# The channel sub-layer's second product by Strassen's seven products of halves for three of four quarters, and squares on ScalarE

## The chip, the cores and the metric

The kernel runs on one core of a Trainium2 chip. The core has five engines with instruction streams of their own, each worked off in order: TensorE (PE, matmuls; its weight loads are shown apart as PEld), VectorE (DVE), ScalarE (ACT), GpSimd (POOL) and SyncE (SP, which issues the DMAs here). SBUF holds tiles of 128 partitions, PSUM the matmul results. The metric is the device time of one execution in microseconds (us).

## The reference

One layer of an encoder over 512 tokens of width 1024: a mixer (a bidirectional state-space branch and a neighbourhood attention, gated and merged), then the channel sub-layer, each with a residual and a LayerNorm. The change concerns the channel sub-layer alone:

```python
def sq_relu_mlp(x, w1, w2):
    return jnp.square(jax.nn.relu(x @ w1)) @ w2
...
h = layer_norm(DN_ALPHA * h + mix, ln1_g, ln1_b)
h = layer_norm(DN_ALPHA * h + sq_relu_mlp(h, w_ff1, w_ff2), ln2_g, ln2_b)
```

`w_ff1` is 1024 x 4096 and `w_ff2` 4096 x 1024, all in float32.

## The kernel before

**Split products.** Every float32 operand is split in two: `hi`, a Copy on ACT into the type fp32r that PE takes, and `lo`, the value minus `hi`, on DVE. A product is three matmuls that accumulate in one PSUM bank, `mm3`: hi x hi (L352), lo x hi (L353), hi x lo (L354). `weights()` and `split_weights()` load 1 MB of weights by one DMA on SP's queue into a raw tile (`ws`) and split it in two halves of 128x1024: hi on ACT (L341, `wh`), lo on DVE (L342, `wl`). `ws`, `wh` and `wl` have two buffers each, so a slab can be prepared while the one before is in use.

**Stages.** First come the LayerNorm of the input, the mixer and its output product `w_o`; then the second LayerNorm writes the 512 tokens into `acc` (four tiles of 128 tokens x 1024) and, transposed, into `h1Th` and `h1Tl` (channels on the partitions, hi and lo). Then the MLP goes over four quarters `fq` of the 4096 inner channels, 1024 each.

**First product of a quarter** (in the code `ff1`): eight inner tiles `f` of 128 channels. Each takes 8 k-steps x 3 matmuls with `w1` as the stationary operand and the 512 tokens as the moving one: 24 matmuls of 512 columns, 192 a quarter. ACT takes the ReLU from PSUM (L1430, `rl`), DVE multiplies it by the bank to square it (L1431), ACT makes `gh`, the hi of the square (L1432), and DVE `gl`, its lo (L1433). In quarter 0 the first four tiles are worked out early, in two halves of 256 tokens, around the second LayerNorm.

**Second product of a quarter** (`ff2`): for two halves of 512 output columns, 4 token tiles x 8 k-steps x 3 matmuls, 192 a quarter, with `gh`/`gl` as the stationary operand and `w2` as the moving one. DVE adds each of the 8 banks to `acc` (L1463 in quarter 0, where it also scales `acc` by ALPHA; L1467 later). The last quarter is written out apart, token tile by token tile, with the last LayerNorm and the output behind each.

**Beside that** POOL applies the second LayerNorm's scale and shift to `acc` (eight operations of 128x1024, L1439); those of tile 0 are tied behind the first inner tiles by a dependency set by hand. Two rows for the last LayerNorm (`row2`) are loaded ahead of the loop.

**Order.** The mixer's order comes from a planner in the code. In the MLP the framework's scheduler orders each engine's stream when the program is built, from the order in which the operations are written, the buffers and its own estimate of durations; on the chip each engine then follows its stream in order and waits on semaphores. So what a stream has behind a waiting instruction waits too.

Of the kernel before, what the change touches and what calls it, by code (L numbers as in the profile page):

```python
# [35 lines left out]
ALPHA = 2.0 ** 0.25  # L36
# [4 lines left out]
BANKS = {"mm": 2, "tr": 2, "cb": 1, "yd": 1, "so": 2}  # L41
# [271 lines left out]
def encoder_layer(ctx, tc, x, w_in, w_attn_br, w_ssd_br, w_o, w_ff1, w_ff2, pcols, rows64,  # L313
                  d_skip, ln_rows, rpb_pad, consts, lmask, out, dbg=None):
    nc = tc.nc
# [30 lines left out]
    def weights(parts, nk, ncol, name, eng=nc.vector, pool=None, after=None):  # L346
        hi = (pool or wp).tile([P, nk, ncol], F32R, tag="wh", name=f"wh_{name}")
        lo = (pool or wp).tile([P, nk, ncol], F32R, tag="wl", name=f"wl_{name}")
        return split_weights(parts, nk, ncol, name, hi, lo, eng, pool, after)

    def mm3(o, lh, ll, rh, rl, start, stop):
        nc.tensor.matmul(o, lh, rh, start=start, stop=False)  # L352
        nc.tensor.matmul(o, ll, rh, start=False, stop=False)  # L353
        nc.tensor.matmul(o, lh, rl, start=False, stop=stop)  # L354
# [49 lines left out]
    gep = ge.__enter__()  # L404
# [41 lines left out]
    op = plan.op  # L446
# [38 lines left out]
    def load_x(t):  # L485
# [7 lines left out]
       r=[(xts[0].name, 0)], w=[(xts[2].name, 0), ("behind", 0)])  # L493
# [838 lines left out]
    def row(i):  # L1332
        r = gep.tile([P, D], F32, tag="gt", bufs=4, name=f"row{i}")
        nc.sync.dma_start(r, ln_rows[i].partition_broadcast(P))
        return r
# [67 lines left out]
    rx0.__exit__(None, None, None)  # L1403


    row2 = [row(4), row(5)]
    ffp = ctx.enter_context(tc.tile_pool(name="ffp", bufs=1, reuse_waits="tile"))
    NQ = D_FF // D
    for fq in range(NQ):
        last = fq == NQ - 1  # L1410
        gh = ffp.tile([P, KD, S], F32R, tag="gh", bufs=2, name=f"gh{fq}")
        gl = ffp.tile([P, KD, S], F32R, tag="gl", bufs=2, name=f"gl{fq}")
        for s in range(4):
            part = [(w_ff1, 0, fq * D + s * 256, 256)]
            if fq == 0 and s == 2:
                w1 = split_weights(part, KD, 256, "f1_0_2", *third(w3p, "f1_0_2"))
            elif fq or s > 1:
                w1 = weights(part, KD, 256, f"f1_{fq}_{s}")
            for j in range(2):
                f = 2 * s + j  # L1420
                if fq == 0 and s < 2:
                    w1, ps = early[f]
                    ff1_half(w1, j, ps, 1)
                else:
                    ps = psx.tile([P, S], F32, tag="mm", bufs=BANKS["mm"], name=f"ps_f1_{fq}_{f}")
                    for k in range(KD):
# [3 lines left out]
                nc.scalar.activation(rl, ps, AF.Relu)  # L1430
                nc.vector.tensor_tensor(out=rl, in0=rl, in1=ps, op=ALU.mult)  # L1431
                nc.scalar.activation(gh[:, f, :], rl, AF.Copy)  # L1432
                ins = nc.vector.tensor_tensor(out=gl[:, f, :], in0=rl, in1=gh[:, f, :].bitcast(F32),  # L1433
                                              op=ALU.subtract)
                if fq == 0 and f == 4:

                    for t in range(NT):
                        for i, o in ((0, ALU.mult), (1, ALU.add)):
                            aff = nc.gpsimd.tensor_tensor(out=acc[t], in0=acc[t], in1=row1[i], op=o)  # L1439
# [5 lines left out]
        def ff2(ps, t, wh, wl, k0):  # L1445

            ts_ = slice(t * P, (t + 1) * P)
            for k in range(4):
                mm3(ps, gh[:, k0 + k, ts_], gl[:, k0 + k, ts_], wh[:, k, :], wl[:, k, :],
                    k0 + k == 0, k0 + k == KD - 1)  # L1450

        if not last:
            for s in range(2):
                cs = slice(s * 512, (s + 1) * 512)
                pss = [psx.tile([P, 512], F32, tag=tag, bufs=BANKS[tag], name=f"ps_f2_{fq}_{s}_{t}")
                       for t, tag in enumerate(("so", "tr", "so", "tr"))]
                for k0 in (0, 4):
                    w2 = weights([(w_ff2, fq * D + k0 * P, s * 512, 512)], 4, 512, f"f2_{fq}_{s}_{k0}")
                    for t in range(NT):
                        ff2(pss[t], t, *w2, k0)  # L1460
                for t in range(NT):
                    if fq == 0:
                        nc.vector.scalar_tensor_tensor(out=acc[t][:, cs], in0=acc[t][:, cs],  # L1463
                                                       scalar=ALPHA, in1=pss[t], op0=ALU.mult,
                                                       op1=ALU.add)
                    else:
                        nc.vector.tensor_tensor(out=acc[t][:, cs], in0=pss[t], in1=acc[t][:, cs],  # L1467
                                                op=ALU.add)
# [89 lines left out]
```

## Time and profile before

| | |
|---|---|
| median of 3 runs | 1220.36 us (1219.28 to 1220.38) |
| profiled execution | 1219.99 us |
| its span (first to last instruction) | 1217.9 us |
| instructions in all | 16716 |
| granted PE clock, mean | 0.993 |
| DMA | 127.19 MB, mean 104 GB/s |
| loads of `w_ff1` and `w_ff2` | 32 of 1024 KB |
| second product, one of the three matmuls (L352, `gh` x `wh`) | x224, 86.3 us busy |

The profile is one execution on the chip. A busy share is the time in which an engine had an instruction running, over the span; an average over stages with different limits. A group of instructions is one line of the code, one operation and one form of tile: its count, the busy time, the mean length of one in ns, and the idle time of its engine just before, with what ended it. A row of the timeline has the start, the length, and in brackets the idle time before it with its releaser. Busy time counts overlapping ends once; mean lengths don't.

### The profile page before, as it was taken

The page shows a single profiled execution, that of the slowest core. Times are in us where ns is not written, and L with a number is a line of the kernel's source. Part 1 is how long each engine was busy: PE and PEld are TensorE (multiplying, and loading weights), DVE is VectorE, ACT ScalarE, POOL GpSimd, SP SyncE. Part 2 cuts the span into 40 slices and gives each one's busy share as a digit, 9 for nine tenths or more (in the row PEclk, how much of TensorE's full clock was granted, in tenths as well). Part 3 has the DMA queues.
Part 4 walks back from the last instruction along what each step waited for, and adds up shares of the span by engine and source line. Part 5 has one row for each costly group of instructions (what it writes and reads, how often), then busy time and mean ns, then how long its engine had stood idle before and what let it go on. Part 6 is the DMA issues. An engine that isn't in the chain of part 4 may idle for free.

```text
span 1217.9 us, 16716 instructions
## 1 busy us (share of the span) xinstructions
PE 1185.8 (97%) x6378; PEld 1017.4 (84%) x6378; DVE 725.7 (60%) x1361; ACT 563.2 (46%) x946; POOL 491.6 (40%) x540
## 2 busy tenths in 40 slices
PE   5999999999999999999999989999999999999996
PEld 5988898989888888788888878899988888888885
DVE  7748475665666665534889874456654433443556
ACT  4576573836456463324677873432241331331510
POOL 1158967777787776203766720024320000000000
PEclk8999999999999999999999999999999999999998
DMA  6144243333324332234332233263114233322401
GB/s 230 53 143 139 90 136 104 120 109 119 110 98 142 113 110 70 69 104 118 83 87 62 70 129 94 90 222 124 36 69 126 81 104 104 104 91 85 160 28 52
DMA packets 124449, 127.19 MB, mean 104 GB/s; under 512 B 22353, under 2 KB 104913, under 8 KB 124369
## 3 DMA queue, kind: packets, MB, share of 16 engines
q1 hardware_dynamic: 124368, 126.13, 33.4%
q8 instruction: 50, 0.82, 0.3%
q14 instruction: 31, 0.25, 0.1%
HBM read 123.88 MB, written 2.23 MB: 104 GB/s over the span
## 4 chain that ended last, share of the span: by engine, by line
PE 88%; DVE 5%; ACT 3%; issue 2%; POOL 1%; DMA 1%; SPq 0%; DVEq 0%; POOLq 0%; ACTq 0%
PE ps_f L354 9%; PE ps_f L352 9%; PE ps_f L353 9%; PE ps_x L352 5%; PE ps_x L354 5%; PE ps_x L353 5%; PE ps_z L352 3%; PE ps_z L353 3%; PE ps_z L354 2%; PE yd L931 2%; PE ps_sbr L352 2%; PE ps_sbr L354 2%; PE ps_sbr L353 2%; PE ps_g L352 2%; PE ps_g L353 2%
## 5 line engine op out<-in xcount | busy, mean ns | idle before, releaser
L341 ACT ACTIVATE wh_f<-ws_f 128x1024 fp32r<-128x1024 f32 x60 | 60.1, 1052 | 118.6 <-PE ps_f L353 96.4
L740 DVE SCALAR_TENSOR_TENSOR cv<-ps_x,pc,cv 128x511 f32<-128x511 f32 (+1 forms) x128 | 95.7, 748 | 25.8 <-ACT cv L732 22.1
L353 PE MATMUL ps_f<-h1Th,wl_f 128*128 128x512 f32 (+1 forms) x288 | 104.6, 366 | 0.0
L352 PE MATMUL ps_f<-h1Th,wh_f 128*128 128x512 f32 (+1 forms) x288 | 104.4, 366 | 0.0
L354 PE MATMUL ps_f<-h1Tl,wh_f 128*128 128x512 f32 (+1 forms) x288 | 103.1, 367 | 1.0 <-DVE h1Tl L428 1.0
L342 DVE TENSOR_TENSOR wl_f<-ws_f,wh_f 128x1024 fp32r<-128x1024 f32 x60 | 72.7, 1251 | 45.3 <-ACT wh_f L341 45.1
L353 PE MATMUL ps_f<-wh_f,gl 128*128 128x512 f32 x224 | 86.8, 389 | 0.0
L354 PE MATMUL ps_f<-wl_f,gh 128*128 128x512 f32 x224 | 86.5, 389 | 0.0
L352 PE MATMUL ps_f<-wh_f,gh 128*128 128x512 f32 x224 | 86.3, 389 | 0.0
L352 PE MATMUL ps_z<-wh_z,hTh 128*128 128x256 f32 x256 | 75.9, 296 | 0.0
L354 PE MATMUL ps_z<-wl_z,hTh 128*128 128x256 f32 x256 | 72.4, 283 | 0.0
L353 PE MATMUL ps_z<-wh_z,hTl 128*128 128x256 f32 x256 | 72.4, 283 | 0.0
L1431 DVE TENSOR_TENSOR rl<-rl,ps_f 128x512 f32<-128x512 f32 x32 | 21.7, 687 | 69.1 <-ACT rl L1430 68.9
L1047 DVE TENSOR_TENSOR ysacc<-ps_sbr,ysacc 128x512 f32<-128x512 f32 x56 | 38.4, 688 | 40.4 <-PE ps_sbr L354 39.9
L354 PEld LDWEIGHTS ps_f<-h1Tl,wh_f 128*128 128x128 f32 x288 | 53.3, 188 | 9.9 <-DVE h1Tl L428 1.2
L352 PEld LDWEIGHTS ps_f<-h1Th,wh_f 128*128 128x128 f32 x288 | 54.1, 188 | 8.9
L353 PEld LDWEIGHTS ps_f<-h1Th,wl_f 128*128 128x128 f32 x288 | 54.2, 188 | 8.6
L1430 ACT ACTIVATE rl<-ps_f 128x512 f32<-128x512 f32 x32 | 19.0, 597 | 89.1 <-PE ps_f L354 85.6
L352 PE MATMUL ps_x<-hTh,wh_bc 128*128 128x512 f32 (+1 forms) x144 | 57.1, 396 | 1.6 <-ACT wh_bc L470 1.6
L352 PE MATMUL ps_sbr<-yTh,wh_sbr 128*128 128x512 f32 x128 | 55.8, 436 | 1.1 <-DVE ysacc L1047 0.5
L353 PE MATMUL ps_x<-hTh,wl_bc 128*128 128x512 f32 (+1 forms) x144 | 54.1, 376 | 2.0 <-POOL wl_bc L473 2.0
L1319 POOL TENSOR_TENSOR gt<-gt,ysacc 128x512 f32<-128x512 f32 x8 | 12.8, 1599 | 106.3 <-ACT gt L1059 98.1
(301 smaller groups left out, 3677.3 us busy)
## 6 DMA issues: line engine op xcount, KB each, us to landing
ws_f<-in_w_ff SPq DMA_DIRECT2D x32, 1024.0 KB
bc<-acs_d SPq DMA_DIRECT2D x32, 512.0 KB
ws_bc<-in_w_in SPq DMA_DIRECT2D x16, 512.0 KB
ws_x<-in_w_in SPq DMA_DIRECT2D x8, 1024.0 KB
ws_z<-in_w_in SPq DMA_DIRECT2D x8, 1024.0 KB
ws_g<-in_w_in SPq DMA_DIRECT2D x8, 1024.0 KB
ws_sbr<-in_w_ssd_br SPq DMA_DIRECT2D x8, 1024.0 KB
ws_qk<-in_w_in SPq DMA_DIRECT2D x16, 512.0 KB
```

Of the source, the lines that this page charges most:

```text
L341: nc.scalar.activation(hi[:, k], st[:, k], AF.Copy)
L342: (eng[i] if isinstance(eng, tuple) else eng).tensor_tensor(out=lo[:, k], in0=st[:, k], in1=hi[:, k].bitcast(F32), op=ALU.subtract)
L352: nc.tensor.matmul(o, lh, rh, start=start, stop=False)
L353: nc.tensor.matmul(o, ll, rh, start=False, stop=False)
L354: nc.tensor.matmul(o, lh, rl, start=False, stop=stop)
L740: op("DVE", 0.75, lambda j=j, o=o, n=n: nc.vector.scalar_tensor_tensor(out=acc()[:, o], in0=ps()[:, n], scalar=tap(j), in1=acc()[:, o], op ...
L931: nc.tensor.matmul(yd()[:, c % 2, h * HD : (h + 1) * HD], bc()[:, 1, h, :], xtok()[:, c, h * HD : (h + 1) * HD], start=True, stop=True)
L1047: op("DVE", 0.69, lambda d=d, ps=ps: nc.vector.tensor_tensor(out=ysacc[:, d, :], in0=ps(), in1=ysacc[:, d, :], op=ALU.add), r=[(ps.name, 0 ...
L1319: nc.gpsimd.tensor_tensor(out=g1, in0=g1, in1=ysacc[:, d, :], op=ALU.mult)
L1430: nc.scalar.activation(rl, ps, AF.Relu)
L1431: nc.vector.tensor_tensor(out=rl, in0=rl, in1=ps, op=ALU.mult)
```

## The change

**Seven products.** For quarters 0 to 2 the second product, a (512 x 1024) times b (1024 x 1024), is cut into halves on all three sides: a(m, i), two token halves and two halves of the inner channels; b(i, n), two inner and two output halves. Eight products of halves are replaced by Strassen's seven, written in the order 3, 6, 4, 2, 1, 5, 7. Each is 4 k-steps x 2 token tiles x 3 matmuls of 512 columns, 24; the bank of a product is added to or subtracted from `acc` at one or two places (`into`, L1492 and L1495): 24 operations a quarter instead of 8, on DVE.

**Left operands.** The square is kept as float32 (`r2`): ReLU on ACT (L1551), then Square on ACT (L1553); `gh` and `gl` are gone. Five of the seven left operands are sums or differences of halves of r2 (`total`, L1438, on DVE, tile `as_`), all seven are split: hi on ACT (L1443), lo on DVE (L1444). They rotate through four pairs of buffers (`blocks`, `wh_blocks`/`wl_blocks`).

**Right operands.** `w2` of a quarter is loaded raw as two tiles of 2 MB by four DMAs (L1427, `w2r_0` and `w2r_1`). Five of the seven right operands are sums (`total`, on POOL, two of 128x1024 each; into tiles `wt_` or in place in `w2r`), all seven are split into `wh` and `wl`, the buffers that the `w1` slabs use too.

**The rest.** `row2` is loaded behind the loop. The last quarter keeps its work.

```diff
+    blocks = ffp.tile([P, 2, 2, 4, 256], F32R, tag="gl", bufs=1, name="blocks")
+    pairs = [(blocks[:, i, 0], blocks[:, i, 1]) for i in range(2)]
...
+    def ff2_strassen(fq, r2):
+        w = [ffp.tile([P, KD, 512], F32, tag="wr", bufs=2, name=f"w2r_{fq}_{n}") for n in range(2)]
...
+        b = {(i, n): w[n][:, 4 * i : 4 * i + 4, :] for i in range(2) for n in range(2)}
+        a = {(m, i): r2[:, 4 * i : 4 * i + 4, m * 256 : (m + 1) * 256] for m in range(2)
+             for i in range(2)}
+        halves = (slice(0, 2), slice(2, 4))
+        def total(dst, x, y, op, eng):
+            for d, k in zip(dst, halves):
+                eng.tensor_tensor(out=d, in0=x[:, k], in1=y[:, k], op=op)
+            return dst
+        def split(hi, lo, src):
+            for x, k in zip(src, halves):
+                nc.scalar.activation(hi[:, k], x, AF.Copy)
+                nc.vector.tensor_tensor(out=lo[:, k], in0=x, in1=hi[:, k].bitcast(F32),
+                                        op=ALU.subtract)
...
+        def left(name, x, y=None, op=ALU.add):
+            hi, lo = pairs[turn[0] % len(pairs)]
+            turn[0] += 1
...
+            t = ffp.tile([P, 4, 256], F32, tag="asum", bufs=1, name=f"as_{fq}_{name}")
+            return split(hi, lo, total(cut(t), x, y, op, nc.vector))
+        def right(name, x, y=None, op=ALU.add, dst=None):
...
+                x = total(cut(dst), x, y, op, nc.gpsimd)
...
+            return split(wp.tile([P, 4, 512], F32R, tag="wh", name=f"wh_f2_{fq}_{name}"),
+                         wp.tile([P, 4, 512], F32R, tag="wl", name=f"wl_f2_{fq}_{name}"), x)
...
+        def product(pss, l, r):
+            for k in range(4):
+                for j, ps in enumerate(pss):
+                    ts_ = slice(j * P, (j + 1) * P)
+                    mm3(ps, l[0][:, k, ts_], l[1][:, k, ts_], r[0][:, k, :], r[1][:, k, :],
+                        k == 0, k == 3)
...
+        product(p3, left("3", a[0, 0]), right("3", b[0, 1], b[1, 1], sub))
+        into(p3, 0, 1)
+        into(p3, 1, 1)
...
+        product(p6, left("6", a[1, 0], a[0, 0], sub), right("6", b[0, 1], b[0, 0], dst=b[0, 1]))
+        into(p6, 1, 1)
...
+        product(p4, left("4", a[1, 1]), right("4", b[1, 0], b[0, 0], sub))
...
+        product(p2, left("2", a[1, 0], a[1, 1]), right("2", b[0, 0]))
...
+        r5 = right("5", b[1, 1])
...
+        product(p1, left("1", a[0, 0], a[1, 1]), right("1", b[0, 0], b[1, 1], dst=b[0, 0]))
...
+        product(p5, left("5", a[0, 0], a[0, 1]), r5)
...
+        product(p7, left("7", a[0, 1], a[1, 1], sub), right("7", b[1, 0], b[1, 1], dst=b[1, 0]))
+        into(p7, 0, 0)
...
                 nc.scalar.activation(rl, ps, AF.Relu)
-                nc.vector.tensor_tensor(out=rl, in0=rl, in1=ps, op=ALU.mult)
-                nc.scalar.activation(gh[:, f, :], rl, AF.Copy)
-                ins = nc.vector.tensor_tensor(out=gl[:, f, :], in0=rl, in1=gh[:, f, :].bitcast(F32),
-                                              op=ALU.subtract)
+                if not last:
+                    ins = nc.scalar.activation(r2[:, f, :], rl, AF.Square)
```

Where the instructions stand now is seen at three places. In the rows an engine's stream is listed in order: line, operation, output <- inputs, and the shape; x2 means two in a row. Lines are those of the changed code.

POOL in quarter 0, where before nothing stood behind the last pair of `acc` (there L1439). The number behind `wt_` is the product, the last number only tells buffers apart:

```order
L1563 TENSOR_TENSOR acc_7632<-acc_7632,row_7621 128x1024
L1438 TENSOR_TENSOR wt_3_0_8672<-w2r_1_8661 128x1024
L1438 TENSOR_TENSOR wt_3_1_8673<-w2r_1_8661 128x1024
L1563 TENSOR_TENSOR acc_7632<-acc_7632,row_7623 128x1024
L1438 TENSOR_TENSOR wt_4_0_8759<-w2r_0_8660 128x1024
L1438 TENSOR_TENSOR w2r_1_8661<-w2r_1_8661,w2r_0_8660 128x1024 x2
L1438 TENSOR_TENSOR wt_4_1_8760<-w2r_0_8660 128x1024
L1438 TENSOR_TENSOR w2r_0_8660<-w2r_0_8660,w2r_1_8661 128x1024 x4
```

The first of these rows still waits for the square of inner tile 4; the ten sums of the quarter's right operands stand between and behind the last two rows of `acc`. The `w2r_1` rows are the right operand of product 6, the `w2r_0` rows those of 7 and 1.

DVE in quarter 0, from the second left operand's sum to the first accumulations (`r_0` is r2 of quarter 0, `wl_f_0_6` the lo of product 6's right operand):

```order
L1438 TENSOR_TENSOR as_2_8799<-r_0_8413 128x512
L1444 TENSOR_TENSOR wl_blocks<-r_0_8413,wh_blocks 128x512
L1444 TENSOR_TENSOR wl_blocks<-as_2_8799,wh_blocks 128x512
L1444 TENSOR_TENSOR wl_f_0_3_8677<-wt_3_0_8672,wh_f_0_3_8676 128x1024
L1444 TENSOR_TENSOR wl_f_0_3_8677<-wt_3_1_8673,wh_f_0_3_8676 128x1024
L1438 TENSOR_TENSOR as_2_8799<-r_0_8413 128x512
L1444 TENSOR_TENSOR wl_blocks<-r_0_8413,wh_blocks 128x512
L1444 TENSOR_TENSOR wl_blocks<-as_2_8799,wh_blocks 128x512
L1438 TENSOR_TENSOR as_1_8848<-r_0_8413 128x512 x2
L1444 TENSOR_TENSOR wl_f_0_6_8722<-w2r_1_8661,wh_f_0_6_8721 128x1024
L1492 SCALAR_TENSOR_TENSOR acc_7632<-acc_7632,ps_f_0_3_0_8666 128x512
L1492 SCALAR_TENSOR_TENSOR acc_7634<-acc_7634,ps_f_0_3_0_8666 128x512
```

The stretch of DVE's stream ahead of the first accumulations before:

```order
L1431 TENSOR_TENSOR rl_5_8605<-rl_5_8605,ps_f_0_5_8580 128x512
L1433 TENSOR_TENSOR gl_8417<-rl_4_8567,gh_8416 128x512
L1433 TENSOR_TENSOR gl_8417<-rl_5_8605,gh_8416 128x512
L1431 TENSOR_TENSOR rl_6_8643<-rl_6_8643,ps_f_0_6_8618 128x512
L1433 TENSOR_TENSOR gl_8417<-rl_6_8643,gh_8416 128x512
L1431 TENSOR_TENSOR rl_7_8673<-rl_7_8673,ps_f_0_7_8648 128x512
L342 TENSOR_TENSOR wl_f_0_0_4_8739<-ws_f_0_0_4_8740,wh_f_0_0_4_8738 128x1024 x2
L1433 TENSOR_TENSOR gl_8417<-rl_7_8673,gh_8416 128x512
L342 TENSOR_TENSOR wl_f_0_1_0_8803<-ws_f_0_1_0_8804,wh_f_0_1_0_8802 128x1024 x2
L1463 SCALAR_TENSOR_TENSOR acc_7632<-acc_7632,ps_f_0_0_0_8678 128x512
```

Ahead of product 6's lo now stand ten operations that read two SBUF tiles, eight of 512 columns and two of 1,024.

PE in quarter 1, where product 5 begins (`ps_f_1_5_0` is its first bank; `wh_f_1_5`, `wh_f_1_1` the right operands):

```order
L354 MATMUL ps_f_1_2_1_9366<-wl_f_1_2_9375,wh_blocks 128x512
L352 MATMUL ps_f_1_5_0_9459<-wh_f_1_5_9408,blocks 128x512
L352 MATMUL ps_f_1_5_1_9460<-wh_f_1_5_9408,blocks 128x512
L352 MATMUL ps_f_1_1_0_9414<-wh_f_1_1_9425,wh_blocks 128x512
L353 MATMUL ps_f_1_1_0_9414<-wh_f_1_1_9425,wl_blocks 128x512
L352 MATMUL ps_f_1_1_1_9415<-wh_f_1_1_9425,wh_blocks 128x512
L353 MATMUL ps_f_1_1_1_9415<-wh_f_1_1_9425,wl_blocks 128x512
L353 MATMUL ps_f_1_5_0_9459<-wh_f_1_5_9408,blocks 128x512
L354 MATMUL ps_f_1_5_0_9459<-wl_f_1_5_9409,blocks 128x512
L353 MATMUL ps_f_1_5_1_9460<-wh_f_1_5_9408,blocks 128x512
L354 MATMUL ps_f_1_5_1_9460<-wl_f_1_5_9409,blocks 128x512
```

Products 5 and 1 are interleaved; before, PE went through one bank after the other with the same three kinds. ACT's stream for the same stretch (`as_5`, `as_7` are left operands, `wh_f_2_0` is `w1` of quarter 2):

```order
L1443 ACTIVATE wh_f_1_5_9408<-w2r_1_9229 128x1024 x2
L1443 ACTIVATE blocks<-as_5_9461 128x512
L1443 ACTIVATE wh_f_1_1_9425<-w2r_0_9228 128x1024 x2
L1443 ACTIVATE blocks<-as_5_9461 128x512
L1443 ACTIVATE blocks<-as_7_9498 128x512 x2
L1443 ACTIVATE wh_f_1_7_9507<-w2r_0_9228 128x1024 x2
L341 ACTIVATE wh_f_2_0_9540<-ws_f_2_0_9542 128x1024 x2
```

Every hi of the late products stands on ACT in the order of this list, and the next quarter's first `w1` behind product 7's.

More of the change, by code (lines that the diff above doesn't have):

```diff
@@ L1360, in ff1_half, with third @@
                 h1Th[:, k, c], h1Tl[:, k, c], k == 0, k == KD - 1)
-    def third(pool, name):
-        return [pool.tile([P, KD, 256], F32R, tag=n, name=f"{n}_{name}") for n in ("wh3", "wl3")]
+    def third(pool, name, shape=[P, KD, 256]):
+        return [pool.tile(shape, F32R, tag=n, name=f"{n}_{name}") for n in ("wh3", "wl3")]
     wos = []
@@ L1403, in encoder_layer, with ff2 @@
     rx0.__exit__(None, None, None)
-    row2 = [row(4), row(5)]
     ffp = ctx.enter_context(tc.tile_pool(name="ffp", bufs=1, reuse_waits="tile"))
     NQ = D_FF // D
+    blocks = ffp.tile([P, 2, 2, 4, 256], F32R, tag="gl", bufs=1, name="blocks")
+    pairs = [(blocks[:, i, 0], blocks[:, i, 1]) for i in range(2)]
+    turn = [0]
+    def ff2(ps, t, wh, wl, k0):
+        ts_ = slice(t * P, (t + 1) * P)
+        for k in range(4):
+            mm3(ps, gh[:, k0 + k, ts_], gl[:, k0 + k, ts_], wh[:, k, :], wl[:, k, :],
+                k0 + k == 0, k0 + k == KD - 1)
@@ L1409, in encoder_layer @@
     for fq in range(NQ):
         last = fq == NQ - 1
-        gh = ffp.tile([P, KD, S], F32R, tag="gh", bufs=2, name=f"gh{fq}")
-        gl = ffp.tile([P, KD, S], F32R, tag="gl", bufs=2, name=f"gl{fq}")
+        if last:
+            gh = ffp.tile([P, KD, S], F32R, tag="gh", bufs=1, name="gh3")
+            gl = ffp.tile([P, KD, S], F32R, tag="gl", bufs=1, name="gl3")
+        else:
+            r2 = ffp.tile([P, KD, S], F32, tag="gh", bufs=1, name=f"r2_{fq}")
         for s in range(4):
@@ L1430, in encoder_layer @@
                 nc.scalar.activation(rl, ps, AF.Relu)
-                nc.vector.tensor_tensor(out=rl, in0=rl, in1=ps, op=ALU.mult)
-                nc.scalar.activation(gh[:, f, :], rl, AF.Copy)
-                ins = nc.vector.tensor_tensor(out=gl[:, f, :], in0=rl, in1=gh[:, f, :].bitcast(F32),
-                                              op=ALU.subtract)
+                if not last:
+                    ins = nc.scalar.activation(r2[:, f, :], rl, AF.Square)
+                else:
+                    nc.vector.tensor_tensor(out=rl, in0=rl, in1=ps, op=ALU.mult)
+                    nc.scalar.activation(gh[:, f, :], rl, AF.Copy)
+                    nc.vector.tensor_tensor(out=gl[:, f, :], in0=rl, in1=gh[:, f, :].bitcast(F32),
+                                            op=ALU.subtract)
                 if fq == 0 and f == 4:
@@ L1443, in encoder_layer @@
                                     reason="behind the first channels")
[L1445 to L1450, printed above, removed]
-        if not last:
[L1453 to L1468, printed above, removed]
+        if not last:
+            if fq == 0:
+                third_pair = third(w3p, "blocks", [P, 2, 4, 256])
+                pairs += [tuple(x[:, i] for x in third_pair) for i in range(2)]
+            ff2_strassen(fq, r2)
     r0 = (NQ - 1) * D
-    w2h = ffp.tile([P, KD, 512], F32R, tag="gh", bufs=2, name="w2h")
-    w2l = ffp.tile([P, KD, 512], F32R, tag="gl", bufs=2, name="w2l")
+    w2h = ffp.tile([P, KD, 512], F32R, tag="wr", bufs=2, name="w2h")
+    w2l = ffp.tile([P, KD, 512], F32R, tag="wr", bufs=2, name="w2l")
     for k0 in (0, 4):
@@ L1477, in encoder_layer @@
              [weights([(w_ff2, r0 + k0 * P, 512, 512)], 4, 512, f"f2_3_1_{k0}") for k0 in (0, 4)]]
+    row2 = [row(4), row(5)]
     for t in range(NT):
```

49 lines of the change are left out of this document (added).

## The prediction, as it was put on record

> **What bounds the kernel now.** I read the page's busy shares and its chain first, then the waits of TensorE (PE) alone over the last part of the program, from 660 us on, which holds the channel sub-layer, and last the windows of that stage.
>
> ```profile
> PE 1185.8 (97%) x6378; PEld 1017.4 (84%) x6378; DVE 725.7 (60%) x1361; ACT 563.2 (46%) x946; POOL 491.6 (40%) x540
> POOL 1158967777787776203766720024320000000000
> PE 88%; DVE 5%; ACT 3%; issue 2%; POOL 1%; DMA 1%; SPq 0%; DVEq 0%; POOLq 0%; ACTq 0%
> PE ps_f L354 <- DVE h1Tl L428: 1.0, 1, 1.0
> 900.00:940.00 40.00, 40.00 (x179) 33.10 (x178) 14.85 (x17) 10.28 (x12) 2.67 (x2) 1.00 0.26 79
> 940.00:980.00 40.00, 40.00 (x178) 33.14 (x177) 16.46 (x21) 11.72 (x16) 0.00 (x0) 1.00 0.34 105
> 953.10 0.60 ACT L1430 ACTIVATE rl<-ps_f 128x512 f32<-128x512 f32 x1 [3.65 <-PE ps_f L354]
> 958.54 0.60 ACT L1430 ACTIVATE rl<-ps_f 128x512 f32<-128x512 f32 x1 [3.46 <-PE ps_f L354]
> ```
>
> PE is busy 97% of the span and makes 88% of the last chain. The digits are POOL's busy tenths in 40 slices of 30.4 us: it does nothing from 913 us on. The wait row is the only one on the MLP's banks (waited, times, longest): 1.0 us, once, at its start. The windows (length, PE, PEld, VectorE (DVE), ScalarE (ACT), GpSimd (POOL), clock, DMA share, GB/s) show PE full at clock 1.00 while DVE works 15 of 40 us. So in the MLP the time is the matmul count times one spacing. Two ReLUs, each behind 24 matmuls, start 5.44 us apart: 0.2267 us per matmul.
>
> **What it removes.** Seven products of 4 k-steps x 2 token tiles x 3 terms are 168 matmuls where a quarter had 192. Three quarters save 72 x 0.2267 = 16.3 us, 5.44 each, all on the path.
>
> As a figure only: the Trainium skill (TensorE: Matmul & The Clock Gate, Back-to-back issue gap) gives about 131 ns for a sustained 512-column matmul. By it the 72 would save 9.4 us and the sum below would end some 7 us later; the two ReLU rows show 226.7 ns here.
>
> **What it adds: prices.**
>
> ```profile
> L342 DVE TENSOR_TENSOR wl_f<-ws_f,wh_f 128x1024 fp32r<-128x1024 f32 x60 | 72.7, 1251 | 45.3 <-ACT wh_f L341 45.1
> L341 ACT ACTIVATE wh_f<-ws_f 128x1024 fp32r<-128x1024 f32 x60 | 60.1, 1052 | 118.6 <-PE ps_f L353 96.4 <-PE ps_o L353 22.1
> L1433 DVE TENSOR_TENSOR gl<-rl,gh 128x512 fp32r<-128x512 f32 x32 | 21.7, 687 | 8.6 <-ACT gh L1432 8.4
> L1432 ACT ACTIVATE gh<-rl 128x512 fp32r<-128x512 f32 x32 | 19.9, 627 | 9.3 <-DVE rl L1431 9.1
> L1467 DVE TENSOR_TENSOR acc<-ps_f,acc 128x512 f32<-128x512 f32 x16 | 11.0, 689 | 22.7 <-PE ps_f L354 22.7
> L1305 POOL TENSOR_TENSOR acc<-acc,rows 128x1024 f32<-128x1024 f32 x2 | 4.8, 2402 | 0.0
> 300.04 5.19 POOL L473 TENSOR_TENSOR wl_bc<-ws_bc,wh_bc 128x1024 fp32r<-128x1024 f32 x2
> 301.32 1.64 DVE L917 TENSOR_TENSOR bc<-bc,amd 128x512 f32<-128x512 f32 x1
> 884.76 3.11 DVE L342 TENSOR_TENSOR wl_f<-ws_f,wh_f 128x1024 fp32r<-128x1024 f32 x1
> 877.07 9.72 POOL L1439 TENSOR_TENSOR acc<-acc,row 128x1024 f32<-128x1024 f32 x4 [20.36 <-PE tp_h L422]
> 883.33 1.28 DVE L1431 TENSOR_TENSOR rl<-rl,ps_f 128x512 f32<-128x512 f32 x2 [1.17 <-ACT rl L1430]
> ```
>
> Busy time over count (60.1 / 60 = 1.00, 72.7 / 60 = 1.21) counts overlapping ends once and is what a step of an unbroken row costs. I take for such a step: DVE 1.18 for a 1,024 lo (some of the 60 were held by POOL), 0.65 for a 512-column sum, lo or accumulation; ACT 1.0 and 0.61; POOL 2.40 for a 1,024 sum. Per quarter the MLP had on DVE 16 lo of weights, 16 half-size squares and lo and 8 accumulations, 16 x 1.18 + 24 x 0.65 = 34.5; it gets 8 lo for w1, 14 lo and 10 sums of r2 halves, 14 lo of w2 and 24 accumulations: 22 x 1.18 + 48 x 0.65 = 57.2, beside 360 x 0.2267 = 81.6 us of PE. ACT goes from 26 to some 40: 22 hi of 1.0, 14 of 0.61, eight ReLU and eight Squares of 0.6. POOL, idle before, gets 10 x 2.40 = 24. That fits as an average; but most of DVE's part is due inside the 38 us of the seven products, and DVE and POOL disturb each other. The left sums read r2 in pieces of 256 columns, which no row of this form shows; the 512-column lo at 0.69 bounds them above, 0.65 is taken.
>
> **Turns.** Two POOL operations with DVE's `bc` between them took 5.19, not 2 x 2.40: 0.39 more; and the 512-column `bc` took 1.64, not 0.65. A lo that started at 884.76 ended at 887.87, 1.08 behind the end of POOL's four (886.79). So a DVE operation with two SBUF inputs waits until a running POOL sum ends, and the next POOL sum waits for it: **they go by turns**. A 512-column one costs POOL 0.4; a 1,024 one 1.18 less the same overlap of 0.25, 0.93 (estimate). DVE operations that read PSUM are not held: at 883.33 two ran in 1.28 during POOL's four. The accumulations are thus free of this, the left sums and all lo are not.
>
> **Quarter 0.**
>
> ```profile
> 883.51 0.40 PE L352 MATMUL ps_f<-h1Th,wh_f 128*128 128x512 f32 x1
> 882.70 1.09 ACT L1430 ACTIVATE rl<-ps_f 128x512 f32<-128x512 f32 x2 [4.96 <-PE ps_f L354]
> L1430 ACT ACTIVATE rl<-ps_f 128x512 f32<-128x512 f32 x32 | 19.0, 597 | 89.1 <-PE ps_f L354 85.6 <-DVE gl L1433 3.5
> ```
>
> Inner tile f4 starts at 883.51; by the new order 90 matmuls lie between it and product 3, 903.9; product 6 is due at 909.35, and its third kind of matmul, which needs the lo of its right sum, four matmuls later, 910.25. POOL's stream begins with acc's last affine pair, behind the Square of f4 on ACT. ACT from 882.70: two ReLU 1.1, two w1 hi 2.0, two Squares 1.2, two ReLU 1.2, four short ones 2.45 and four more 2.45 with that Square: 893.1. Ahead of right 6's lo, DVE's order has ten two-SBUF operations (eight of 512 columns, two of 1,024), and POOL has ten operations ready (the pair of acc, two sums each of right 3, 4 and 6, and right 7's two, which wait only for POOL itself): 10 x 2.40 + 8 x 0.4 + 2 x 0.93 = 29.1, so 922.2. The lo ends at 923.4, PE has it 0.1 later: **13.25 late** for 910.25. Behind that lo stand, on DVE, the accumulations of product 3 and the lo of left 1 and right 4; only PE waits for them, later than for this one, since PE itself stands. From there PE and DVE run side by side, DVE late again at three places. The second half of right 6's lo stands behind four accumulations and a left lo: 923.4 + 2.6 + 0.65 + 1.18 = 927.9, due 16 matmuls on, 927.1: +0.8. Then DVE has 5.6 us of right 4, left 1, left 5's sums and product 6's accumulations (933.4), right 2 2.36, left 5's two lo around one POOL turn for right 1's sum 0.65 + 2.4 + 0.65, product 4's four accumulations 2.6, and right 5's lo 1.18: 943.2, where PE comes at 940.6: +2.7. Right 1's lo by the same count: 949.5 for 948.65, +0.85. Lag of quarter 0: **17.6**. From below it is 2, if the turns let right 6 through: seven POOL sums before it end the sixth at 907.5, and 1.0 + 1.2 for hi and lo give 909.7.
>
> **Quarters 1 and 2.** POOL's sums lie in the 43 us of the first product there, in which DVE has 8 lo of w1 (9.4) and some 11 of the first products' halves; I take them as hidden. With t = 0 at product 3's start, DVE's work is unbroken from 5.65 (first accumulation): 4 accumulations 2.60, one lo 0.65, right 4 2.36, left 1 sums 1.30, 2 accumulations 1.30, right 2 2.36, left 1 lo 1.30 with one POOL turn 2.40, 4 accumulations 2.60, half of left 5's sum 0.65: 23.17. Its hi on ACT ends at 23.8, product 5 is due at 4 x 5.44 = 21.76: **+2.0**. Right 1's hi stands behind it on ACT, 24.8, and PE, two matmuls on, wants it at 24.2: +0.6. Then DVE: right 5's lo 2.36, the sum's other half 0.65, left 5's lo 0.65: 26.8, four matmuls on was 25.7, +1.1; product 2's four accumulations 2.60 and right 1's lo 1.18, 30.6, twelve matmuls on was 29.6, +1.0. Product 7's right hi needs the wh slot of product 5, which the new order of PE ends last, directly before product 7: ACT 1.0 and the handover, +1.3. The next quarter's first w1 hi stands behind product 7's two hi on ACT, while PE has four matmuls (0.9) to spare: 2.05, +1.15. Sum **7.15** a quarter, 14.3 for two; from below 4.9 if DVE keeps up with products 5 and 1, from above 12 if the turns also hold back w1's lo.
>
> **What is hidden.** Eight Squares per quarter cost ACT 0.60 each in place of a Copy of 0.63; DVE's multiply goes; both lie beside 43 us of PE. No Square is in the trace: between 0.60 and 0.69, eight times, nothing either way.
>
> ```profile
> 932.00:933.00 1.00, 1.00 (x6) 0.81 (x6) 0.00 (x0) 0.00 (x0) 0.00 (x0) 1.00 1.02 342
> 933.00:934.00 1.00, 1.00 (x6) 0.84 (x5) 0.00 (x0) 0.00 (x0) 0.00 (x0) 1.00 0.95 337
> 715.00:720.00 5.00, 2.28 (x16) 1.77 (x15) 2.61 (x12) 2.81 (x5) 0.23 (x1) 1.00 0.14 51
> 720.00:725.00 5.00, 5.00 (x16) 3.94 (x15) 5.00 (x9) 5.00 (x9) 0.00 (x0) 0.66 0.92 352
> ```
>
> The 4 MB of raw w2 per quarter move at 340 GB/s, 12.3 us, within 43 of the first product; the w1 slab behind them in SP's queue keeps 6 us or more. If that cover went, it would be 3 us a slab. Behind a pause PE runs slower for a while: the window after 715 to 720 has 16 matmuls at clock 0.66, where 24 would fit, 1.8 us. After quarter 0's pause DVE sets the pace, so I add 0 (to 1). The last quarter keeps its work; row2's later load has tens of us.
>
> Sum, from this execution's 1219.99 (span 1217.9 and 2.1 around it; the median shown is 0.4 more): -16.3 + 17.6 + 14.3 = +15.6, **1236**.
>
> **Rivals.** *The sums get out of the way* (faster): no more than 2 in quarter 0 and 4.9 in each other, 11.8 - 16.3 = -4.5, 1215.5; all of it hidden, 1203.7. For it: POOL idles for the whole MLP after its affine, and DVE half of it. Against: ten turns ahead of one lo, in DVE's fixed order. It is decided by right 6's lo, before or after 910.25. *The turns reach the first product* (slower still): in quarters 1 and 2 eight POOL sums fall among w1's lo, f4's and f6's, with a slack near one turn; +5 each, 1246. For it: DVE is held 2.4 at a time; against: PE is then 24 matmuls per tile behind. *Cancelled*: quarter 0 loses about as much as the two floors allow, lag 16.3, 1220. That the saving is not made is out: the order has 168 matmuls a quarter.
>
> **How the numbers follow.** Forecast 0.48, faster 0.27 (1204 to 1217), cancelled 0.10, slower still 0.15. The forecast alone would be 1229 to 1241. The range, 1211 to 1246, leaves out the lower part of the faster case and what lies above the slowest. A measurement of this kernel tells 0.2%, 2.4 us, from no change: faster 0.27, same 0.09, slower 0.64.
>
> **What would show it.** In the profile after: a wait of PE of some 13 us in quarter 0 near 910 on DVE's lo of right 6 (L1444), DVE and POOL rows there alternating with held lengths of 2.4 and more; waits of 1 to 2 us in each later quarter at products 5, 1 and 7; spacing still 0.2267. Wrong if POOL's sums and DVE's lo overlap at their short lengths, if right 6 is ready in time, or if the first products of quarters 1 and 2 wait.

## The result, and the profile after

The changed kernel takes 1232.40 us (median of 5 runs, 1228.54 to 1235.33) where the kernel before took 1220.38 beside it; the ratio is 1.0091, 95% interval 1.0072 to 1.0111. It is **slower by 12 us** (0.9%), though it has 72 matmuls fewer. Its profiled execution took 1232.32, with a span of 1230.5. The page's lines that answer to those of before:

```profile
PE 1177.5 (96%) x6306; PEld 1004.0 (82%) x6306; DVE 836.4 (68%) x1451; ACT 605.4 (49%) x1006; POOL 579.1 (47%) x570
POOL 1158968777787776204766700043391612702000
PE 76%; DVE 16%; ACT 3%; issue 3%; DMA 1%; POOL 0%; SPq 0%; DVEq 0%; ACTq 0%; POOLq 0%
```

PE has its 72 matmuls less (6306 for 6378), DVE 111 us more of busy time (in which its waiting for POOL counts), and POOL now works behind 913 us, where it had been idle. In the last chain DVE went from 5% to 16%. PE's waits from 884 us on, which were 1.0 us in all before (waited, times, longest), first those of quarter 0, then those of quarters 1 and 2:

```profile
PE ps_f L354 <- DVE wl_f L1444: 10.1, 3, 9.4
PE ps_f L352 <- ACT wh_f L1443: 1.8, 1, 1.8
PE ps_f L352 <- DVE acc L1492: 1.5, 2, 1.1
PE ps_f L354 <- DVE h1Tl L428: 1.1, 1, 1.1
...
PE ps_f L352 <- ACT rl L1551: 1.3, 1, 1.3
PE ps_f L354 <- DVE wl_f L1444: 1.0, 2, 0.5
PE ps_f L353 <- DVE wl_blocks L1444: 0.7, 1, 0.7
PE ps_f L353 <- DVE blocks L1444: 0.7, 1, 0.7
...
```

One wait stands out: 9.4 us for a right operand's lo, in quarter 0. To size the whole I take the stage from the start of inner tile f4 to the last matmul, since what lies ahead of it has the same instructions in the same order in both kernels and yet ended between 881.5 and 886.9 in the profiles of this study. In the timeline (start, length), the last matmul of before, then both ends of after:

```profile
1208.37 0.39 PE L354 MATMUL ps_f<-wl_f,gh 128*128 128x512 f32 x1
...
885.20 0.40 PE L352 MATMUL ps_f<-h1Th,wh_f 128*128 128x512 f32 x1
1220.91 0.39 PE L354 MATMUL ps_f<-wl_f,gh 128*128 128x512 f32 x1
```

The stage took 1208.37 - 883.51 = 324.86 before and 335.71 after, 10.85 more; 1.7 of the span's 12.6 lie ahead of it, where nothing was changed. With the saving of 16.3 made, PE lost 27.2 us in it. Summing what each row of PE starts later than the matmuls ahead of it explain at 0.2267 each: 18.9 in quarter 0, 3.3 in the products of quarter 1, 1.6 at one ReLU in the first product of quarter 2, 3.3 in its products.

**The turns.** POOL, DVE and PE in quarter 0, and last POOL and DVE in quarter 1:

```profile
894.07 2.48 POOL L1563 TENSOR_TENSOR acc<-acc,row 128x1024 f32<-128x1024 f32 x1 [5.61 <-ACT r L1553]
896.51 5.66 POOL L1438 TENSOR_TENSOR wt<-w2r 128x1024 f32<-128x1024 f32 x2
917.13 5.54 POOL L1438 TENSOR_TENSOR w2r<-w2r,w2r 128x1024 f32<-128x1024 f32 x2
...
899.84 2.89 DVE L1444 TENSOR_TENSOR wl_blocks<-as,wh_blocks 128x512 fp32r<-128x512 f32 x1
902.65 6.75 DVE L1444 TENSOR_TENSOR wl_f<-wt,wh_f 128x1024 fp32r<-128x1024 f32 x2
917.75 5.48 DVE L1438 TENSOR_TENSOR as<-r 128x512 f32<-128x512 f32 x2
923.15 1.21 DVE L1444 TENSOR_TENSOR wl_f<-w2r,wh_f 128x1024 fp32r<-128x1024 f32 x1
...
924.41 1.22 PE L354 MATMUL ps_f<-wl_f,blocks 128*128 128x512 f32 x2 [9.36 <-DVE wl_f L1444]
943.19 0.47 PE L352 MATMUL ps_f<-wh_f,blocks 128*128 128x512 f32 x1 [1.10 <-DVE acc L1492]
...
1020.39 6.83 POOL L1438 TENSOR_TENSOR w2r<-w2r,w2r 128x1024 f32<-128x1024 f32 x2 [32.71 <-DVE wl_f L1444]
1021.30 1.29 DVE L1444 TENSOR_TENSOR wl_blocks<-as,wh_blocks 128x512 fp32r<-128x512 f32 x2
1022.50 2.47 DVE L1495 TENSOR_TENSOR acc<-acc,ps_f 128x512 f32<-128x512 f32 x4
```

From 897 on each 512-column sum or lo of DVE takes 2.7 to 2.9 us as long as POOL has sums. Accumulations, which read PSUM, are not held: in quarter 1 four of them take 2.47, 0.6 each, while POOL's two sums run. POOL's ten end at 917.13 + 5.54 = 922.67, 28.6 after they began; the next DVE row, right 6's lo, takes 1.21, and PE goes on as it ends. The window of that quarter's seven products (length, PE, PEld, DVE, ACT, POOL, clock, DMA share, GB/s):

```profile
905.60:962.60 57.00, 43.56 (x170) 33.61 (x169) 56.79 (x53) 19.91 (x25) 23.20 (x8) 0.85 0.18 63
```

PE works 43.6 of 57.0 us in it and DVE, its waiting for POOL counted as busy, 56.8.

### The profile page after: what moved, and what is told of

It reads as the page before. It is cut to its first block, busy times and chain, and to the rows that moved or that the text cites. A ratio compares the mean times of both kernels' runs of the same rounds, so it can differ in the third digit from the quotient of the medians.

```text
span 1230.5 us, 16770 instructions
## 1 busy us (share of the span) xinstructions
PE 1177.5 (96%) x6306; PEld 1004.0 (82%) x6306; DVE 836.4 (68%) x1451; ACT 605.4 (49%) x1006; POOL 579.1 (47%) x570
## 4 chain that ended last, share of the span: by engine, by line
PE 76%; DVE 16%; ACT 3%; issue 3%; DMA 1%; POOL 0%; SPq 0%; DVEq 0%; ACTq 0%; POOLq 0%
PE ps_f L354 7%; PE ps_f L352 7%; PE ps_f L353 7%; PE ps_x L352 5%; PE ps_x L354 5%; PE ps_x L353 4%; DVE wl_f L1444 3%; PE ps_z L352 3%; PE ps_z L353 2%; PE ps_z L354 2%; PE yd L931 2%; PE ps_sbr L352 2%; PE ps_sbr L354 2%; PE ps_sbr L353 2%; PE ps_g L352 2%
## 5 line engine op out<-in xcount | busy, mean ns | idle before, releaser
L1438 POOL TENSOR_TENSOR w2r<-w2r,w2r 128x1024 f32<-128x1024 f32 x18 | 56.2, 3147 | 77.6 <-DVE wl_f L1444 77.6
L342 DVE TENSOR_TENSOR wl_f<-ws_f,wh_f 128x1024 fp32r<-128x1024 f32 x36 | 51.0, 1447 | 20.1 <-ACT wh_f L341 20.1
L352 PE MATMUL ps_x<-hTh,wh_x 128*128 128x512 f32 (+1 forms) x144 | 55.1, 383 | 0.0
L1438 POOL TENSOR_TENSOR wt<-w2r 128x1024 f32<-128x1024 f32 x12 | 31.7, 2665 | 49.3 <-DMA w2r<-in_w_ff 49.3
L354 PE MATMUL ps_x<-hTl,wh_bc 128*128 128x512 f32 (+1 forms) x144 | 54.2, 376 | 0.2 <-DVE hTl L585 0.2
L341 ACT ACTIVATE wh_f<-ws_f 128x1024 fp32r<-128x1024 f32 x36 | 36.1, 1052 | 36.8 <-PE ps_o L353 22.1
L473 POOL TENSOR_TENSOR wl_bc<-ws_bc,wh_bc 128x1024 fp32r<-128x1024 f32 x15 | 37.5, 2518 | 35.3 <-ACT wh_bc L470 35.2
```

What stands on the lines that cost most here:

```text
L341: nc.scalar.activation(hi[:, k], st[:, k], AF.Copy)
L342: (eng[i] if isinstance(eng, tuple) else eng).tensor_tensor(out=lo[:, k], in0=st[:, k], in1=hi[:, k].bitcast(F32), op=ALU.subtract)
L473: op(e, us, lambda k=k, eng=eng: eng.tensor_tensor(out=wl()[:, k], in0=ws()[:, k], in1=wh()[:, k].bitcast(F32), op=ALU.subtract), r=keys + ...
L1438: eng.tensor_tensor(out=d, in0=x[:, k], in1=y[:, k], op=op)
```

## The experiments

Each kernel was timed beside the kernel before on the same chip, and the table has its stage as above, from its own profile. "Saved" is 0.2267 per matmul left out, "lost" is the stage less 324.86 and more the saving. The stage varies less than the time: two profiles of one kernel (eight_dve_p1 and eight_dve_p1_again) took 1213.10 and 1210.29, and have it at 316.37 and 316.45.

| run | time, before beside it | ratio, 95% | stage | saved | lost |
|---|---|---|---|---|---|
| the change | 1232.40, 1220.38 | 1.0072 to 1.0111 | 885.20 to 1220.91: 335.71 | 16.3 | 27.2 |
| q0_sums_dve | 1225.69, 1220.86 | 1.0028 to 1.0055 | 885.98 to 1216.67: 330.69 | 16.3 | 22.1 |
| affine_early | 1232.23, 1220.86 | 1.0063 to 1.0117 | 883.90 to 1219.39: 335.49 | 16.3 | 26.9 |
| q0_no_sums | 1218.31, 1220.86 | 0.9950 to 0.9981 | 886.85 to 1210.61: 323.76 | 16.3 | 15.2 |
| q0_eight | 1225.22, 1220.86 | 1.0014 to 1.0040 | 881.50 to 1211.01: 329.51 | 10.9 | 15.5 |
| eight_late | 1217.80, 1221.65 | 0.9956 to 0.9980 | 884.15 to 1206.44: 322.29 | 10.9 | 8.3 |
| eight_late_p1 | 1213.22, 1221.65 | 0.9913 to 0.9950 | 885.20 to 1203.10: 317.90 | 10.9 | 3.9 |
| eight_dve_p1 | 1210.99, 1221.65 | 0.9892 to 0.9929 | 885.30 to 1201.67: 316.37 | 10.9 | 2.4 |
| squares_alone | 1221.68, 1221.65 | 0.9989 to 1.0013 | 884.66 to 1209.52: 324.86 | 0 | 0 |
| seven_dve_p1 | 1218.40, 1220.94 | 0.9966 to 0.9989 | 884.16 to 1206.85: 322.69 | 16.3 | 14.1 |
| after_p1 | 1227.06, 1220.94 | 1.0030 to 1.0064 | 881.60 to 1211.58: 329.98 | 16.3 | 21.4 |

**Quarter 0's sums on DVE** (`sums` stands in `right` where `nc.gpsimd` stood):

```diff
+        sums = nc.vector if fq == 0 else nc.gpsimd
```

> The ten right sums of quarter 0 go from POOL to DVE, nothing else in the text; DVE gets 10 x 1.2 = 12 us more in that quarter and shares nothing with POOL there. Theory (turns): PE's 9.4 us wait for right 6's lo goes, since without turns its lo follows its sums at once, near 912; the quarter's lag falls from 19 to 3 to 5 us: 1217 (1214 to 1221). Rival (DVE is simply overfull): 12 us more on DVE make the quarter later still, 1232 to 1244. If the turns matter but DVE is as full, between: 1224 to 1230.

1225.69, in the band between the two. PE's two largest waits in this kernel's MLP:

```profile
PE ps_f L352 <- ACT blocks L1444: 5.0, 2, 4.6
PE ps_f L354 <- DVE wl_f L1445: 2.6, 4, 1.0
```

No lo is waited for by more than 1.0, and the stage is 5.0 us shorter although DVE does ten operations more; but left 5, whose sum stands behind all of DVE's other work, is now 4.6 late. So the turns did cost, and DVE is full too.

**The affine pair earlier**

```diff
+                if fq == 0 and f == 0:
+                    first = ins
...
-                                tc.add_manual_dep(aff.ins, ins.ins.name, mybir.DependencyInfo(
+                                tc.add_manual_dep(aff.ins, first.ins.name, mybir.DependencyInfo(
```

> The dependency that holds acc's last affine pair, and with it all sums behind it in POOL's stream, is tied to inner tile f0 in place of f4: POOL starts at about 888.8 in place of 894.1, with the same ten operations. Theory (the lo of right 6 comes when ten turns are through): all of the 5.3 us come off PE's wait, 1227 (1225.5 to 1229). Rival (the last left sums wait for inner tile f7 at 906.5 and five turns are due behind it, whenever POOL starts): under 1 us, 1231.5 to 1233.

1232.23, the rival's number, but by neither mechanism. PE's waits in quarter 0 of this kernel, the row of the second wait, and DVE rows:

```profile
PE ps_f L352 <- ACT wh_f L1443: 5.9, 2, 5.4
PE ps_f L354 <- DVE wl_f L1444: 3.8, 1, 3.8
PE ps_f L352 <- ACT rl L1551: 2.3, 2, 2.0
...
917.84 0.80 PE L354 MATMUL ps_f<-wl_f,blocks 128*128 128x512 f32 x1 [3.83 <-DVE wl_f L1444]
...
891.51 2.87 DVE L1438 TENSOR_TENSOR as<-r 128x512 f32<-128x512 f32 x1
902.69 2.89 DVE L1444 TENSOR_TENSOR blocks<-r,blocks 128x512 fp32r<-128x512 f32 x1
916.57 2.35 DVE L1444 TENSOR_TENSOR wl_f<-wt,wh_f 128x1024 fp32r<-128x1024 f32 x2
920.04 1.21 DVE L1444 TENSOR_TENSOR wl_f<-w2r,wh_f 128x1024 fp32r<-128x1024 f32 x1
```

The waits have moved from product 6 to product 3, which begins 5.4 late for its right hi and then, at its third matmul, waits 3.8 for its right lo (the one made from `wt`). Right 6's lo (from `w2r`, at 920.04) comes while PE is still in product 3, and nobody waits for it. For the turns now hit the lo of left 3 and the sums and lo of left 6, six operations that in the changed kernel ran in 0.68 each just ahead of POOL's stream. Nine operations of left operands and right lo are held in either kernel, only not the same nine.

**Quarter 0 without right sums**

```diff
-            if y is None:
+            if y is None or fq == 0:
                 x = cut(x)
```

> Quarter 0's five right sums are left out (the raw halves of w2 are split in their place), so neither POOL nor DVE does them; all matmuls, splits and accumulations stay. Theory (turns): quarter 0 has no POOL operation beside acc's affine, right 6 is ready ahead of PE, lag 1 to 4 us: 1215 (1213 to 1218); against the run with the sums on DVE it shows what these cost there. Rival (DVE's own splits, left sums and accumulations are the quarter's limit): the lag stays above 10 us, 1224 or more.

1218.31, 0.3 above the theory's range, and the rival falls. This kernel leaves the sums out and so computes something else; it serves for the time alone. The stage is 335.71 - 323.76 = 11.95 us shorter than the change's and 6.9 shorter than with the sums on DVE: over the stage the ten sums cost PE 12 us on POOL and 7 on DVE. Quarter 0 itself still loses 5.0 without them, by the rows of PE, where 1 to 4 were expected.

**Quarter 0 with eight products**

```diff
+        plain = fq in (0, NQ - 1)
...
+        if fq == 0:
...
+                    for t in range(NT):
+                        ff2(pss[t], t, *w2, k0)
```

> Quarter 0 is done with eight products as before the change, quarters 1 and 2 with seven. Theory: quarter 0's 19 us of lag go and its 5.4 us of saving with them, the other two quarters keep theirs (3 and 4.5 of lag, 10.9 saved): 1232.4 - 13.6 = 1219 (1216.5 to 1221). Rival (whichever quarter comes first with seven products meets POOL's sums late): the loss moves to quarter 1, 1226 or more.

1225.22, a miss by 6: quarter 0 lost 7 us with the plain code. Quarters 1 and 2 lost 8.2 as in the change, so the loss did not move there, as the rival has it. The scheduler had put POOL's first sums for quarter 1 ahead of `acc`'s last pair:

```profile
884.75 6.71 POOL L1437 TENSOR_TENSOR wt<-w2r 128x1024 f32<-128x1024 f32 x2
...
885.79 10.03 DVE L342 TENSOR_TENSOR wl_f<-ws_f,wh_f 128x1024 fp32r<-128x1024 f32 x3
...
896.48 0.80 PE L353 MATMUL ps_f<-wh_f,gl 128*128 128x512 f32 x1 [4.58 <-DVE gl L1557]
```

Three lo of `w1`, 3.4 us without turns, took 10.03, and the lo of the square came 4.6 us late for PE. The next run holds these sums back:

```diff
+                if fq == 1 and eng is nc.gpsimd:
+                    tc.add_manual_dep(o.ins, ins.ins.name, mybir.DependencyInfo(
```

> Quarter 0 with eight products, as in q0_eight, and POOL's sums for quarter 1 are held until quarter 0's last lo is done (there they ran into it: PE waited 4.6 us for gl at 896.5 and ran slow behind it). Theory (turns): that wait and what follows it go, some 6 us: 1219 (1217.5 to 1221). Rival (the sums only meet other work later, w1's lo of quarter 1): the wait comes back there, 1224 or more.

1217.80: that wait and all loss in quarter 0 are gone (8.3 lost where 15.5 were). The prediction for it is met.

**Product 1's right sum in tiles of its own**

```diff
-        product(p1, left("1", a[0, 0], a[1, 1]), right("1", b[0, 0], b[1, 1], dst=b[0, 0]))
+        product(p1, left("1", a[0, 0], a[1, 1]), right("1", b[0, 0], b[1, 1]))
```

> As eight_late, and product 1's right sum goes to tiles of its own in place of being written over w2, so POOL makes it early and no longer between left 1's two lo. Theory (turns): DVE gains the 2.4 us that POOL held it there, and PE's waits where products 5 and 1 begin (2.6 us in each of quarters 1 and 2) shrink to under 1: 1215.5 (1214 to 1217). Rival (these waits come from the amount of DVE's own work between products 3 and 5): as eight_late, 1218 to 1220.

1213.22, 0.8 below the theory's range; 4.4 us of the stage went, 2.2 a quarter of the 3.3 lost there. Left 5's sum, 2.87 long in eight_late, takes 0.68: most of the waits at products 5 and 1 were one POOL turn. The same edit on the changed kernel:

> The changed kernel with one edit: product 1's right sum in tiles of its own, made early; POOL keeps all sums. Theory: quarters 1 and 2 gain what eight_late_p1 gained on eight_late, 2.2 us each, quarter 0 keeps its wait for right 6 and its ten turns: 1228 (1226 to 1229.5). Rival (the tiles of their own hold up POOL's stream, since their buffers come free with products 3 and 4): no gain, 1232.

1227.06, within its range: 5.7 us of the stage. Quarters 1 and 2 give 4.2 of them, for 4.4 expected. The rest is in quarter 0: PE's wait for right 6's lo grew from 9.4 to 11.5, as POOL now has twelve operations in a row, but the waits and slow matmuls that the change has from 943 to 949 are gone.

**All right sums of quarters 1 and 2 on DVE, product 1's in tiles of its own**

```diff
+        sums = nc.vector if True else nc.gpsimd
```

> Quarter 0 with eight products; quarters 1 and 2 with all right sums on DVE, product 1's in tiles of its own; POOL does nothing behind acc's affine. DVE gets 10 x 1.14 = 11.4 us more a quarter. Theory (turns are what costs, DVE has room in the first products): no wait of 4.6, none of 1.3 for ReLU, at most 3 us at products 5 and 1: 1217 (1215 to 1219). Rival (DVE overfull in the products): its waits there grow by half of the 11.4 each, 1224 or more.

1210.99, which misses the range on its fast side. PE's waits behind the second LayerNorm in this kernel have one row left in the MLP beside the 1.1 us on h1Tl:

```profile
PE ps_f L352 <- ACT wh_f L1443: 1.1, 2, 0.5
```

DVE took the sums, 11.4 us a quarter by the estimate above, without loss, since none of them stands in the products. The windows of quarter 1's seven products, first with the sums on POOL (eight_late_p1), then in this kernel:

```profile
992.66:1032.36 39.70, 39.12 (x172) 31.72 (x170) 37.79 (x51) 19.80 (x25) 0.00 (x0) 1.00 0.20 64
992.77:1032.51 39.74, 39.19 (x172) 31.75 (x170) 37.83 (x51) 19.80 (x25) 0.00 (x0) 1.00 0.19 65
```

DVE has the same 51 operations there. Timed again:

> The same kernel as eight_dve_p1, timed in more rounds: 1211 (1209.5 to 1212.5), 0.9% under the kernel before.

1211.67 beside 1220.94, ratio 0.9932 (0.9919 to 0.9946), 0.7% under the kernel before. This version is faster than both kernels.

**The same with seven products in quarter 0 too**

> The changed kernel, seven products in all three quarters, with all right sums on DVE and product 1's in tiles of its own: no POOL sum at all. Quarters 1 and 2 as in eight_dve_p1 (2.4 us of lag together). Theory (quarter 0's rest is DVE's own work, 12 us of lag with the sums on DVE, some 2 less without the in-place wait): 10 us of lag against 5.4 saved, so 1211.0 + 4.6 = 1215.5 (1213 to 1218). Rival (with the turns gone quarter 0 is as free as the others): lag under 3, 1207 to 1209.

1218.40, 0.4 above the theory's range, and the rival falls: without any POOL sum quarter 0 still loses 11.8 us by the rows of PE, more than the 10 expected. Windows of this kernel (length, PE, PEld, DVE, ACT, POOL, clock, DMA share, GB/s): first product and seven products of quarter 0, then of quarter 1:

```profile
884.20:904.60 20.40, 20.40 (x93) 16.87 (x92) 19.24 (x16) 13.95 (x23) 8.97 (x4) 1.00 0.17 52
904.60:954.40 49.80, 44.01 (x169) 34.10 (x168) 47.57 (x60) 19.84 (x24) 0.00 (x0) 0.90 0.24 81
954.40:998.00 43.60, 43.60 (x194) 36.08 (x194) 27.32 (x29) 19.55 (x28) 0.00 (x0) 1.00 0.33 101
998.00:1037.60 39.60, 39.05 (x171) 31.64 (x170) 37.73 (x51) 19.79 (x24) 0.00 (x0) 1.00 0.18 64
```

In quarter 0 only four of the eight inner tiles are left when the stage begins, 20.4 us to do in what quarter 1 does in 43.6. So nine operations and 9.8 us of DVE more fall into the products (47.57 for 37.73), and the products take 49.8 for 39.6.

**The squares alone** (the kernel before, with the multiply of quarters 0 to 2 on ScalarE):

```diff
-                nc.vector.tensor_tensor(out=rl, in0=rl, in1=ps, op=ALU.mult)
+                if fq < NQ - 1:
+                    nc.scalar.activation(rl, rl, AF.Square)
+                else:
+                    nc.vector.tensor_tensor(out=rl, in0=rl, in1=ps, op=ALU.mult)
```

> The kernel before with one part of the change alone: in quarters 0 to 2 the square is ScalarE's Square in place of DVE's multiply; eight products everywhere. Theory (hidden beside PE): as before within 1.5 us, 1219.5 to 1222. Rival (ACT's chain ReLU, Square, Copy delays the second product's first operand): 0.6 us a quarter at the most, 1222.5.

1221.68 beside 1221.65, and the stage is 324.86 as before: this part is free.

## Why the prediction was right, and where its sizes were off

The direction, the place and the mechanism held: +12.0 measured for +15.6 forecast, of which 10.85 lie in the stage that the sum is about.

**The saving** was made: the rows of PE outside the waits keep their spacing, and 6378 - 6306 = 72.

**Quarter 0**, 17.6 forecast, 18.9 measured. The stream of POOL began at 894.07 in an execution that was 1.69 later at f4, that is 0.7 earlier than worked out, ran 28.6 for 29.1, and PE's wait ended at 924.41, 0.8 ahead of 923.5 + 1.69. Up to there 12.0 were lost (0.5 for right 3's lo, 2.0 for right 6's hi, 9.5 for its lo), for 13.25; the waits behind it came to 2.4 for 4.35, and 0.9 is spread over small delays. The rest, 3.6, is the clock, which I had put at 0 to 1 because DVE would set the pace. So that the two totals lie so close is partly luck: this term, left out, made up for waits that I had too long by 3.2. (The window from which I took the clock's price has room for 22 matmuls, not 24; no term of the sum rests on that.) Two windows of the slow stretches:

```profile
926.00:927.00 1.00, 1.00 (x4) 0.81 (x3) 1.00 (x3) 0.00 (x0) 0.00 (x0) 0.50 0.00 0
947.00:948.00 1.00, 1.00 (x4) 0.71 (x4) 1.00 (x3) 0.85 (x2) 0.00 (x0) 0.50 0.54 37
```

At clock 0.50 each matmul starts 0.43 behind the one ahead, 0.2 more than at 1.00; in two stretches, behind 924.4 and behind 945.4, that made 2.0 and 1.6.

**Quarters 1 and 2**, 14.3 forecast, 8.2 measured: this is where the sum was too high. In quarter 1:

```profile
1024.89 2.87 DVE L1438 TENSOR_TENSOR as<-r 128x512 f32<-128x512 f32 x1
...
1027.80 0.63 ACT L1443 ACTIVATE blocks<-as 128x512 fp32r<-128x512 f32 x1 [3.34 <-DVE as L1438]
1039.51 2.01 ACT L1443 ACTIVATE wh_f<-w2r 128x1024 fp32r<-128x1024 f32 x2 [1.01 <-PE ps_f L353]
...
1011.36 2.48 DVE L1495 TENSOR_TENSOR acc<-acc,ps_f 128x512 f32<-128x512 f32 x4
1013.75 0.68 DVE L1444 TENSOR_TENSOR wl_blocks<-as,wh_blocks 128x512 fp32r<-128x512 f32 x1
```

The chain is the one that was forecast, with one POOL turn in it, at left 5's sum. But from product 3's start at 1006.10 to the end of that sum it has 1024.89 + 2.87 - 1006.10 = 21.66 where I had 23.17: four accumulations take 1013.75 - 1011.36 = 2.39, 0.60 each, for the 0.65 taken from group means, and the first begins 5.26 behind product 3, not 5.65. So the four delays at products 5 and 1 are 0.6, 0.4, 0.8 and 0.6 for 2.0, 0.6, 1.1 and 1.0, with waits of PE of 0.2 to 0.7 where 1 to 2 were to be seen. Of the two terms behind them the 1.3 is not there at all, and of the 1.15 there is 0.2: **the step that failed is "Product 7's right hi needs the wh slot of product 5, which the new order of PE ends last"**. Product 7's two hi began at 1039.51, behind product 1's last matmul (1039.26), while ten of product 5's were still to come, up to 1041.5; so it was not product 5's slot that they waited for. The next quarter's first `w1` hi, right behind them, held PE by 0.2 at 1042.84. These two terms are 2.25 a quarter too high, the four delays 2.2; small delays of 0.6 a quarter and the ReLU's 1.6 below went the other way, so that the sum was too high by 6.1 there.

**Hidden parts.** Squares cost nothing (324.86 for 324.86), the raw loads of w2 delayed no matmul. The sums of quarters 1 and 2, taken as hidden in the first product, were nearly so: one ReLU stood on ACT behind the hi of a left operand whose sum DVE had to wait a turn for, and PE waited 1.3 at 1070.73. A wait in the first product of a later quarter was one of the signs by which the prediction was to be wrong; it came once.

**The rivals.** That the sums get out of the way ended on the other side of its own point: right 6's lo was late, at 924.4. What the runs add is how near this rival was: with quarter 0's right sums left out altogether the stage is 323.76, just under that of before, and with eight products there and the rest on DVE the time is 1211. That turns reach the first product was real but 1.6 in one quarter, not 5 in each. q0_eight shows it in full where the scheduler lets sums meet `w1`'s lo: 4.6 us.

## What to carry to other kernels

Work that is moved off PE must be counted on the engines that get it within the stage where it is due, not over the span: here 16 us of matmuls went, and DVE, at 60% of the span before, was taken for 56.8 of the 57 us in which quarter 0's products should have run in 38. An idle POOL is no free helper for a DVE that has two SBUF inputs in nearly every operation: in quarter 0 a sum on POOL held a DVE operation of 0.60 until it ended, 2.7 to 2.9 us in all, and the ten sums on DVE were cheaper for PE (7 us for 12). A cut in matmuls pays where the extra operations find idle time ahead of it, as in quarters 1 and 2 with 43 us of first product, and not in quarter 0 with 20.

## What the runs showed of the hardware that I had not expected

The clock fell to half without one long pause. Windows of the change around the start of the 9.4 us wait, in the same columns as above:

```profile
914.90:915.10 0.20, 0.15 (x1) 0.00 (x0) 0.20 (x2) 0.00 (x0) 0.20 (x1) 0.60 0.00 0
915.10:924.30 9.20, 0.00 (x0) 0.00 (x0) 9.17 (x5) 3.50 (x5) 7.57 (x3) 0.50 0.00 0
```

PE worked until 915.05, and the clock was down already at 914.9 to 915.1, behind waits of 0.3 and 1.8 us that ended at 909.46 and 913.86; behind the 9.4 us it stayed at 0.50 for 4 us. It was 0.50 again from 946 to 949, behind waits of 1.1, 0.4 and 0.4 us within 3.5 us, in which PE was busy about half of the time. In seven_dve_p1 it was 0.50 from 914.6 to 917.9, behind one wait of 1.6 us that ended at 914.29. Four waits of 0.2 to 0.7 us between 1028 and 1035 were not followed by slow matmuls. Where the point lies between these was not tried.

The turns are not strict. In the quarter 1 rows above, POOL's two sums for product 1 take 6.83 where 2 x 2.40 is their length alone: the first began at 1020.39 and stood for some 2 us, while DVE ran both lo of left 1 behind it at their short length (1.29 for the two). POOL's second sum followed the first at once, as DVE was reading PSUM, and left 5's sum waited for that one alone. What decides who goes first was not tried.
